# Expert blocks of a mixture-of-experts stage repacked by strips of 32 rows, with the next block's transposes moved to the middle of a block

## The chip, the cores and the metric

The kernel runs on one core of a Trainium2 chip. The metric is the device time of one execution in microseconds (us). Matmuls and transposes run on TensorE (PE in the profile), elementwise work on VectorE (DVE) and ScalarE (ACT), gathers and scatters of rows are issued by GpSimd (POOL), and SyncE (SP) issues the plain DMAs, the weight tiles among them, in the order of its program.

## The reference

Two transformer blocks in float32, one after the other, on 512 tokens of width 1024. The first ends in a mixture of experts, which is the stage that the change touches:

```
scores = sigmoid(h @ router_w)                        # 512 x 64
top_idx = top 6 of 64 experts, groups limited         # 3072 places
top_w = scores[top_idx] / sum * ROUTED_SCALE
for each expert e, over the tokens that chose it:
    y[tok] += top_w * ((silu(h @ w_gate[e]) * (h @ w_up[e])) @ w_down[e])
out = x + gt2 * (routed + swiglu(h, s_gate, s_up, s_down))   # the shared expert
```

The second block (state-space mixer, then a squared-relu MLP) follows and is not touched.

## The kernel before

**Places and blocks.** The 512 x 6 choices are sorted by expert into blocks of 128 row places. Four experts (60 to 63) have a fixed block each, blocks n = 0 to 3. The other 60 are ranked by load on the chip; a table `CAPS` says at compile time how many rows rank r may have. Ranks 0 to 17 stand alone (ranks 0, 1 and 2 over two blocks each), ranks 18 to 43 share a block in pairs (strips of 64 rows), ranks 44 to 59 in fours (strips of 32). That makes 42 blocks, whose order is that of `BLOCKS`, made by `plan()`: singles and shared blocks are interleaved. Rows beyond an expert's cap go to overflow blocks (`beyond`), of which there are none with these inputs.

**One block** (`ffn`): the block's 128 rows are gathered from DRAM into one of three buffers X; eight transposes (`pt_x` q = 0 and 1, four each) turn them, and `modulate` writes them as xT; 8 steps of matmuls make `gu` (512 columns) from weight tiles 0 and 1 of each expert, one matmul per strip and step; ACT and DVE make h; two transposes `pt_h`, and ACT copies them to hT; the matmuls `py` (two halves, two steps each) use weight tile 2; DVE multiplies into y, and POOL scatters y's rows, adding to `yacc` in DRAM. In the trace a block's tiles carry a b: gub, hb, pt_hb, pyb. Each float32 matmul is two records there, so a block with one expert has 16 gub and 8 pyb records, a pair 32 and 16, a four 64 and 32.

**Strips.** Where experts share a block, each has its own columns of the array by `tile_position=(0, a)`, a being the strip's first row.

**Weights.** Each expert is three tiles of 1024 KB (`ewrank` 0, 1, 2 and, by slot, `ewx`; the first four experts `ewfix`), which SP loads in block order into a ring of 10 to 13 slots, not before the slot's last reader is done, and with at most eight in flight (`load`). For the last `LEAVE` = 6 blocks three slots leave the ring.

**Hooks.** The shared expert's matmuls stand after the pyb of fixed block numbers: su, sg, su after n = 10, 11, 12, and `spy` after n = 13 to 16. After n = 17 the constants of the next stage are loaded (`row_g_final`, `sbc`, `ssd`) into space that slots of the ring held, and DVE computes with them.

**Order.** The order of instructions on an engine is decided by a scheduler unless the PE queue is pinned; SP runs its DMAs in program order.

Of the kernel before, what the change touches and what calls it, by code (L numbers as in the profile page):

```python
# [7 lines left out]
F32 = mybir.dt.float32  # L8
# [8 lines left out]
P = 128  # L17
# [809 lines left out]
def block_one(k, pool, early, two, route):  # L827
# [7 lines left out]
    with ExitStack() as es:  # L835
# [217 lines left out]
NE = 64  # L1053
NFIX = 4
NRK = NE - NFIX
NPAIR, NQUAD = 18, 44
CAPS = [256, 192, 152, 128, 124, 118, 108, 100, 92, 88, 86, 82, 79, 76, 75, 72, 70, 68, 64, 64, 62, 62, 59, 57, 56, 54, 54, 52, 51,
        50, 49, 46, 45, 44, 44, 43, 42, 41, 41, 40, 39, 38, 37, 37, 32, 32, 32, 31, 30, 30, 28, 26, 25, 23, 22, 20, 20, 18, 17, 16]
CAPS = [-(-c // 16) * 16 for c in CAPS]
NOV = 72  # L1060
LEAVE = 6
LAST = 0
AHEAD = 2
RING = 10
RINGX = 3

# [3 lines left out]

def plan():

    fixed = [(e, P, [("fix", NRK + e)]) for e in range(NFIX)]
    one, more, b, r = [], [], NFIX, 0
    while r < NRK:
        n = 1 if r < NPAIR else 2 if r < NQUAD else 4
        c = CAPS[r]
        if n == 1:
            g = []
            while c > 0:  # L1080
                g.append((b, min(c, P), [("rank", r)]))
                c -= P
                b += 1
            one.append(g)
        else:
            more.append([(b, P, [("rank", r + i) for i in range(n)])])
            assert max(CAPS[r:r + n]) <= P // n
            b += 1
        r += n

    more = more[::-1]
    m = len(one) - LAST
    order, i, j = [], 0, 0
    while i < m or j < len(more):
        if i >= m or j < len(more) and j * m <= i * len(more):
            order.append(more[j])
            j += 1
        else:
            order.append(one[i])
            i += 1  # L1100
    order += one[m:]
    return fixed + [x for g in order for x in g], b


BLOCKS, NB = plan()
NBT = NB + NOV
NSLOT = NB * P
STEP = [-(-c // P) * P if r < NPAIR else 64 if r < NQUAD else 32 for r, c in enumerate(CAPS)] + [P] * NFIX
CST2 = ["iota", "low", "col", "base", "cap"]


def const2():
    j = np.arange(P)[:, None]
    i = np.arange(P)[None, :]
    t = {
        "iota": np.broadcast_to(i, (P, P)),
        "low": (j < i),
        "col": np.broadcast_to(j, (P, P)),

        "base": np.broadcast_to(np.resize(np.concatenate([NFIX * P + np.cumsum([0] + STEP[:NRK - 1]), np.arange(NFIX) * P]), P)[:, None], (P, P)),  # L1120
        "cap": np.broadcast_to(np.resize(np.array(CAPS + [P] * NFIX), P)[:, None], (P, P)),
    }
    return np.concatenate([np.asarray(t[n], np.float32) for n in CST2], 1)
# [22 lines left out]
class Moe:  # L1146
# [332 lines left out]
    def fixed(self, ps, pp):  # L1479

        k, nc, rp = self.k, self.k.nc, self.rp
        V = nc.vector
        pl = rp.tile([P, 4, NFIX], F32, name="fx_pl")
        V.tensor_tensor(pl, pp[:, 0:4, NRK:NE], self.M[:, :, NRK:NE], ALU.mult)
        pt = ps.tile([P, NFIX, 4], F32, tag="tp", name="fx_tab")
        for e in range(NFIX):
            oh = self.part_of(512 * e, 4, P)
            V.tensor_tensor(oh, self.iota1.unsqueeze(1).to_broadcast([P, 4, P]), pl[:, :, e:e + 1].to_broadcast([P, 4, P]), ALU.is_equal)
            for t in range(4):
                nc.tensor.matmul(pt[:, e, :], oh[:, t, :], self.tv[:, t, e, :], start=(t == 0), stop=(t == 3))  # L1490
# [91 lines left out]
    def gather(self, idx):

# [5 lines left out]
                                            bounds_check=511, oob_is_err=False)  # L1589
        return X  # L1590

    def ffn(self, pool, ps, ws, X, wslot, n, nm):

        k, nc = self.k, self.k.nc
        xT = pool.tile([P, 8, P], F32, tag="xT", name="xT" + nm)
        for q in range(2):
            pt = ps.tile([P, 4, P], F32, tag="tp", name=f"pt_x{nm}{q}")
            for i in range(4):
                nc.tensor.transpose(pt[:, i, 0:n], X[0:n, (4 * q + i) * P:(4 * q + i + 1) * P], k.ident[0:n, 0:n])
            self.modulate(pt[:, :, 0:n], q, lambda c: xT[:, c, 0:n])  # L1600
        m = n // len(ws)
        parts = [(i * m, (i + 1) * m) for i in range(len(ws))]
        gu = ps.tile([P, 512], F32, tag="gu", name="gu" + nm)
        for i in range(8):
            for (a, b), w in zip(parts, ws):
                nc.tensor.matmul(gu[a:b, :], xT[:, i, a:b], w[i // 4][:, (i % 4) * 512:(i % 4) * 512 + 512],
                                 start=(i == 0), stop=(i == 7), **({"tile_position": (0, a)} if len(ws) > 1 else {}))
        sg = pool.tile([P, 256], F32, tag="sg", name="sg" + nm)
        nc.scalar.activation(sg[0:n], gu[0:n, 0:256], AF.Silu)  # L1609
        h = pool.tile([P, 256], F32, tag="h", name="h" + nm)  # L1610
        nc.vector.scalar_tensor_tensor(h[0:n], gu[0:n, 256:512], wslot[0:n], sg[0:n], ALU.mult, ALU.mult)  # L1611
        pt = ps.tile([P, 2, P], F32, tag="tp", name="pt_h" + nm)
        for c in range(2):
            nc.tensor.transpose(pt[:, c, 0:n], h[0:n, c * P:(c + 1) * P], k.ident[0:n, 0:n])
        hT = pool.tile([P, 2, P], F32, tag="hT", name="hT" + nm)
        nc.scalar.copy(hT[:, :, 0:n], pt[:, :, 0:n])
        y = pool.tile([P, 1024], F32, tag="y", name="y" + nm, bufs=3)
        for half in range(2):
            cs = slice(512 * half, 512 * half + 512)
            py = ps.tile([P, 512], F32, tag="py", name=f"py{nm}{half}")  # L1620
            for c in range(2):
                for (a, b), w in zip(parts, ws):
                    nc.tensor.matmul(py[a:b, :], hT[:, c, a:b], w[2][:, c * 1024 + half * 512:c * 1024 + half * 512 + 512],
                                     start=(c == 0), stop=(c == 1), **({"tile_position": (0, a)} if len(ws) > 1 else {}))
            nc.vector.tensor_tensor(y[0:n, cs], py[0:n], self.gt2[0:n, cs], ALU.mult)  # L1625
        return y

    def scatter(self, y, parts):

        for a, idx in parts:  # L1630
# [3 lines left out]
                                                in_=y[a:a + n], in_offset=None, bounds_check=511, oob_is_err=False,  # L1634
                                                compute_op=ALU.add)

    def blocks(self, bp, ps, hooks, span):

        pend, Xs = self.pend, self.Xs
        for n in range(*span):  # L1640
            b, rows, whos = BLOCKS[n]
            if n == len(BLOCKS) - LEAVE:
                for f in self.first:
                    self.slots.remove(f)
            if n == len(BLOCKS) - LAST:

                last = [self.load(w[0]) for _, _, w in BLOCKS[n:]]
                for i in ((0, 1), (2,)):
                    for w in last:
                        for j in i:  # L1650
                            w[1](j)
            ws = self.load_block(whos)
# [8 lines left out]
        if span[1] == len(BLOCKS):  # L1661
            for q in pend:
                self.scatter(*q)
            self.beyond(bp, ps)

    def beyond(self, bp, ps):
        k, nc, tc = self.k, self.k.nc, self.k.tc
        V = nc.vector
        n = nc.values_load(self.nov, min_val=0, max_val=NOV)
        with tc.For_i(0, n, 1) as i:  # L1670
# [747 lines left out]
def body(nc, tc, I, out, dbg=None):  # L2418
# [3 lines left out]
    with ExitStack() as es:  # L2422
# [11 lines left out]
        with ExitStack() as e1:  # L2434
            moe.es.close()
            moe.more_ring(e1, pool)
            bp = pool(e1, "moeb", 2)
            moe.Xt = [bp.tile([P, 1024], F32, name=f"X{i}", bufs=1) for i in range(AHEAD + 1)]
# [3 lines left out]
            for _, _, whos in BLOCKS[:3]:  # L2442
                moe.load_block(whos)
# [32 lines left out]
```

## Time and profile before

| | |
|---|---|
| three runs | 2032.37, 2032.55 and 2033.91 us |
| median | 2032.55 us |
| profiled execution | 2032.14 us |
| its span | 2030.3 us |
| mean granted clock of TensorE | 0.958 |
| PE busy | 1827.9 us (90%) |
| expert blocks, n = 4 to 41, on PE | 648.02 to 1215.35 us |
| bytes moved | 394.01 MB |

The span begins with the first instruction of the profiled execution and ends with the last; the profiled execution's own time is 1.84 us longer than its span. Times of the trace are counted from the span's start. The expert stage is some 30% of the span.

### The profile page before, as it was taken

How to read it: one execution, taken by the hardware profiler on the slowest of the kernel's cores; microseconds unless marked ns; L12 is line 12 of the kernel's file. 1: busy time of each engine (PE TensorE's matmuls, PEld its weight loads, DVE VectorE, ACT ScalarE, POOL GpSimd, SP SyncE). 2: the span in 40 equal slices, each digit the busy share in tenths (PEclk: the TensorE clock that was granted, in tenths of full speed). 3: DMA queues.
4: the chain of work that ended last, by engine and by line, in shares of the span. 5: the costliest groups of instructions: out<-in, count | busy, mean ns of one | idle time of the engine just before them, and what ended most of it. 6: DMA issues, size and time to landing. Idle time of an engine off the chain costs nothing. (4 is left out here: it accounts for less than half of the span.)

```text
span 2030.3 us, 24186 instructions
## 1 busy us (share of the span) xinstructions
PE 1827.9 (90%) x8465; PEld 1235.3 (61%) x8465; DVE 995.1 (49%) x2205; ACT 596.5 (29%) x1124; POOL 503.4 (25%) x408
## 2 busy tenths in 40 slices
PE   5997778987889999989999984999999999999998
PEld 3785556876644333333333333888888788888886
DVE  4789955667866222352222226667433453323352
ACT  5443311213323111111111114343323334323441
POOL 1314343542322221212121215333100113101300
PEclk9998888997979999999999996999999999999999
DMA  8354353226478999999999973333332432333241
GB/s 309 122 184 148 89 161 97 81 71 215 157 295 297 354 370 351 346 392 389 365 369 370 374 267 114 122 94 92 108 99 84 134 100 94 93 94 104 78 140 42
DMA packets 135569, 394.01 MB, mean 194 GB/s; under 512 B 46932, under 2 KB 59348, under 8 KB 109080
## 3 DMA queue, kind: packets, MB, share of 16 engines
q1 hardware_dynamic: 109608, 363.60, 50.6%
q0 software_dynamic: 12016, 27.29, 5.5%
q10 hardware_dynamic: 13824, 1.58, 0.5%
q8 instruction: 67, 1.10, 0.2%
q14 instruction: 54, 0.44, 0.1%
HBM read 365.13 MB, written 39.06 MB: 199 GB/s over the span
## 5 line engine op out<-in xcount | busy, mean ns | idle before, releaser
L139 PE MATMUL gub<-ewrank,xTb 128*64 128x512 f32 (+5 forms) x960 | 266.4, 595 | 0.8 <-DMA ewrank<-ew 0.2
L274 DVE TENSOR_TENSOR wlo<-wraw,whi 128x1024 fp32r<-128x1024 f32 (+1 forms) x103 | 120.9, 1174 | 138.4 <-ACT whi L273 137.5
L139 PEld LDWEIGHTS gub<-ewrank,xTb 128*64 128x64 f32 (+5 forms) x960 | 89.0, 140 | 159.5 <-issue 146.7
L273 ACT CAST whi<-wraw 128x1024 fp32r<-128x1024 f32 (+1 forms) x115 | 113.9, 991 | 211.9 <-PE psi L139 50.6
L139 PE MATMUL pyb<-ewrank,hTb 128*64 128x512 f32 (+5 forms) x440 | 154.6, 609 | 3.3 <-DMA ewrank<-ew 1.3
L139 PE MATMUL psi<-xnh,whi 128*128 128x512 f32 (+1 forms) x368 | 142.6, 388 | 0.0
L139 PE MATMUL psi<-xnl,whi 128*128 128x512 f32 (+1 forms) x368 | 141.1, 384 | 0.0
L1633 POOL DMA_INDIRECT yacc<-yb,tok x63 | 89.0, 1412 | 171.3 <-DVE yb L1625 121.5
L1611 DVE SCALAR_TENSOR_TENSOR hb<-gub,tw,sgb 128x256 f32<-128x256 f32 (+5 forms) x38 | 18.3, 482 | 230.8 <-ACT sgb L1609 230.8
L1335 ACT ACTIVATE xTb<-pt_xb,B,A 128x128 f32<-128x128 f32 (+5 forms) x168 | 74.1, 445 | 170.3 <-DVE xTb L1337 169.0
L139 PE MATMUL psi<-xnh,wlo 128*128 128x512 f32 (+1 forms) x296 | 113.2, 383 | 0.0
L1587 POOL DMA_INDIRECT X<-hrow,tok x38 | 39.5, 1041 | 292.0 <-PE pt_xb L142 286.4
L1337 DVE TENSOR_SCALAR xTb<-pt_xb,A,B 128x128 f32<-128x128 f32 (+5 forms) x168 | 65.6, 393 | 89.3 <-PE pt_xb L142 52.9
L2399 POOL TENSOR_TENSOR fr<-fr 128x512 f32<-128x512 f32 x32 | 48.6, 1519 | 238.2 <-ACT fr L2398 238.2
L139 PE MATMUL psf<-xml,whi 128*128 128x512 f32 (+1 forms) x272 | 102.5, 377 | 0.2 <-DVE xml L274 0.2
L139 PE MATMUL psf<-xmh,whi 128*128 128x512 f32 (+1 forms) x272 | 102.4, 377 | 0.2 <-ACT xmh L273 0.2
L139 PE MATMUL psf<-xmh,wlo 128*128 128x512 f32 (+1 forms) x272 | 102.4, 377 | 0.0
L1609 ACT ACTIVATE sgb<-gub 128x256 f32<-128x256 f32 (+5 forms) x42 | 16.0, 382 | 262.4 <-PE gub L139 262.4
L139 PEld LDWEIGHTS pyb<-ewrank,hTb 128*64 128x64 f32 (+5 forms) x440 | 46.7, 143 | 76.0 <-issue 64.7
L1625 DVE TENSOR_TENSOR yb<-pyb,gt 128x512 f32<-128x512 f32 (+5 forms) x84 | 58.0, 690 | 70.2 <-PE pyb L139 70.0
L139 PEld LDWEIGHTS psi<-xnh,whi 128*128 128x128 f32 x368 | 69.9, 191 | 13.8 <-ACT xnh L2264 0.4
L139 PEld LDWEIGHTS psi<-xnl,whi 128*128 128x128 f32 x368 | 70.0, 190 | 13.2
(752 smaller groups left out, 4026.0 us busy)
## 6 DMA issues: line engine op xcount, KB each, us to landing
ewrank<-ew SPq DMA_DIRECT2D x168, 1024.0 KB, 25.1
wraw<-w_in SPq DMA_DIRECT2D x59, 512.0 KB, 3.6
wraw<-ff SPq DMA_DIRECT2D x32, 512.0 KB, 3.5
wf<-ff SPq DMA_DIRECT2D x64, 256.0 KB, 2.7
wm<-w_mod SPq DMA_DIRECT2D x28, 512.0 KB, 7.8
ewfix<-ew SPq DMA_DIRECT2D x12, 1024.0 KB, 15.4
ewx<-ew SPq DMA_DIRECT2D x12, 1024.0 KB, 20.2
wm<-w_mod SPq DMA_DIRECT2D x10, 1024.0 KB, 6.2
```

Of the source, the lines that this page charges most:

```text
L139: return self._done(self.eng.matmul(out, lhsT, rhs, **kw), rate, rhs)
L273: nc.scalar.copy(hi, raw)
L274: (eng or nc.vector).tensor_tensor(lo, raw, hi.bitcast(F32), ALU.subtract)
L1335: nc.scalar.activation(dst(c), pt[:, i, :], AF.Identity, scale=sa, bias=sb)
L1337: nc.vector.tensor_scalar(dst(c), pt[:, i, :], sa, sb, ALU.mult, ALU.add)
L1587: self.k.nc.gpsimd.indirect_dma_start(out=X[0:idx.shape[0]], out_offset=None, in_=self.hrow, in_offset=bass.IndirectOffsetOnAxis(ap=idx, a ...
L1609: nc.scalar.activation(sg[0:n], gu[0:n, 0:256], AF.Silu)
L1611: nc.vector.scalar_tensor_tensor(h[0:n], gu[0:n, 256:512], wslot[0:n], sg[0:n], ALU.mult, ALU.mult)
L1625: nc.vector.tensor_tensor(y[0:n, cs], py[0:n], self.gt2[0:n, cs], ALU.mult)
L1633: self.k.nc.gpsimd.indirect_dma_start(out=self.yacc[self.nsc % 2], out_offset=bass.IndirectOffsetOnAxis(ap=idx, axis=0), in_=y[a:a + n], i ...
L2399: nc.gpsimd.tensor_tensor(r, r, r, ALU.mult)
```

## The change

**Packing.** Caps are multiples of 32: ranks 0 to 2 have 256, 192 and 160 rows, ranks 3 to 7 128, ranks 8 to 17 96, ranks 18 to 43 64, ranks 44 to 59 32. A rank of 96 shares its block with one of 32; as strips these are 64, 32 and 32 rows, the first two of one expert (three-strip blocks). Rank 1's last 64 rows share a block with rank 2's first 64, and rank 2's last 96 with rank 44. That leaves 39 blocks. Experts, weight tiles (64 times three), and the 3072 places are the same; the number of gathers falls from 42 to 39, and the row scatters stay at 67.

**Order of blocks.** After the fixed four: n = 4 one expert of 32 rows; 5, 6 rank 0; 7 a four; 8, 9 pairs; 10 to 12 ranks 1 and 2; 13 to 16 pairs; 17 rank 3; 18 to 20 pairs; 21 rank 4; 22 to 25 pairs; 26 rank 5; 27 to 29 three-strip; 30 rank 6; 31 to 34 three-strip; 35 rank 7; 36 to 38 three-strip. The hooks keep their block numbers. Up to n = 17 there are now 78 tiles to load, not 84, and for n from 18 on 114, not 108.

**Transposes.** The first four `pt_x` of block n + 1 are issued ahead of block n's `pt_h`, the other four behind it. PE runs in program order for the blocks from n = 2 on. Rows are gathered one block further ahead, with the same three buffers.

```
-NPAIR, NQUAD = 18, 44
+STRIPS = [8, 6, 5] + [4] * 5 + [3] * 10 + [2] * 26 + [1] * 16
+CAPS = [32 * s for s in STRIPS]
-NOV = 72
+NOV = 73
-AHEAD = 2
+AHEAD = 3
...
+    few += [group([0]), group([1, 2] + ones(1))] + [group([r]) for r in range(3, n4)]
+    for n in (3, 2, 1):
+        while any(STRIPS[r] == n for r in todo):
+            g = [r for r in todo if STRIPS[r] == n][:{3: 1, 2: 2, 1: 4}[n]]
+            many.append(group(g + (ones(1) if n == 3 else [])))
...
+    def turn(self, ps, xT, X, n, nm, q):
+        pt = ps.tile([P, 4, P], F32, tag="tp", name=f"pt_x{nm}{q}")
+        for i in range(4):
+            self.k.nc.tensor.transpose(pt[:, i, 0:n], X[0:n, (4 * q + i) * P:(4 * q + i + 1) * P], self.k.ident[0:n, 0:n])
+        return lambda: self.modulate(pt[:, :, 0:n], q, lambda c: xT[:, c, 0:n])
...
+        strips = [(a + i, min(a + m, a + i + s), w) for (a, m, _), w in zip(parts, ws)
+                  for i, s in ([(0, 64), (64, 32)] if m == 96 else [(0, m)])]
...
+        put = then.pop(0)() if then else None
         pt = ps.tile([P, 2, P], F32, tag="tp", name="pt_h" + nm)
         for c in range(2):
             nc.tensor.transpose(pt[:, c, 0:n], h[0:n, c * P:(c + 1) * P], k.ident[0:n, 0:n])
         hT = pool.tile([P, 2, P], F32, tag="hT", name="hT" + nm)
         nc.scalar.copy(hT[:, :, 0:n], pt[:, :, 0:n])
+        if put:
+            put()
+            then.pop(0)()()
...
+        self.k.nc.tensor.pin = span[0] > 0
...
+            nxt, xT = self.block_turns(bp, ps, n + 1) if n + 1 < len(BLOCKS) else ((), None)
+            y = self.ffn(bp, ps, ws, self.xT, (self.twf if n < NFIX else self.tw)[:, b:b + 1], rows, parts, f"b{b}", nxt)
```

How it moves PE's rows, first in a pair. Before, PE, from the `pt_h` of one pair block to the gub of the block after it:

```order
L142 MATMUL pt_hb35_7084<-cst_60,hb35_7082 128x128 x2
L142 MATMUL pt_xb140_7125<-cst_60,X0_4565 128x112 x4
L142 MATMUL pt_xb141_7134<-cst_60,X0_4565 128x112
L139 MATMUL pyb350_7090<-ewrank38_2_7037,hTb35_7087 64x512
L139 MATMUL pyb351_7096<-ewrank38_2_7037,hTb35_7087 64x512
L142 MATMUL pt_xb141_7134<-cst_60,X0_4565 128x112 x2
L139 MATMUL pyb350_7090<-ewrank39_2_7039,hTb35_7087 64x512
L139 MATMUL pyb350_7090<-ewrank38_2_7037,hTb35_7087 64x512
```

With the change, the same place of a pair block (ranks 40 and 41):

```order
L142 MATMUL pt_xb60_5615<-cst_60,X1_4566 128x128 x4
L142 MATMUL pt_hb35_5620<-cst_60,hb35_5613 128x128 x2
L142 MATMUL pt_xb61_5629<-cst_60,X1_4566 128x128 x4
L139 MATMUL pyb350_5639<-ewrank40_2_5586,hTb35_5623 64x512
L139 MATMUL pyb350_5639<-ewrank41_2_5588,hTb35_5623 64x512
L139 MATMUL pyb350_5639<-ewrank40_2_5586,hTb35_5623 64x512
L139 MATMUL pyb350_5639<-ewrank41_2_5588,hTb35_5623 64x512
L139 MATMUL pyb351_5645<-ewrank40_2_5586,hTb35_5623 64x512
```

The transposes of the next block left the pyb matmuls and stand around `pt_h`, and the two experts' strips alternate throughout, where two matmuls of one strip had followed each other.

A three-strip block with the change, PE, the first steps of gub and its middle (rank 9 with 96 rows, rank 46 with 32):

```order
L139 MATMUL gub15_8699<-ewrank9_0_8683,xTb15_8590 64x512
L139 MATMUL gub15_8699<-ewrank9_0_8683,xTb15_8590 32x512
L139 MATMUL gub15_8699<-ewrank46_0_8685,xTb15_8590 32x512
L139 MATMUL gub15_8699<-ewrank9_0_8683,xTb15_8590 64x512
L139 MATMUL gub15_8699<-ewrank9_0_8683,xTb15_8590 32x512
```

Before, PE, in a block with one expert of that size class:

```order
L139 MATMUL gub14_7143<-ewrank7_0_7115,xTb14_7124 112x512 x4
L139 MATMUL gub14_7143<-ewrank7_1_7117,xTb14_7124 112x512 x4
L142 MATMUL pt_hb14_7156<-cst_60,hb14_7154 128x112 x2
L142 MATMUL pt_xb340_7212<-cst_60,X1_4566 128x128 x4
L139 MATMUL pyb140_7162<-ewrank7_2_7119,hTb14_7159 112x512 x2
```

Where one matmul per step used the columns of the whole block, three now use 64, 32 and 32 of them, and a block has 24 gub matmuls instead of 8.

On SP, before, around the loads for the next stage (`row_g_final` to `ssd`) behind the tiles of n = 17:

```order
L1519 DMA ewrank5_2_6401<-ew 128x2048
L1728 DMA row_g_final_6459<-g_final 128x1024
L1820 DMA sbc_6469<-sbc 128x1024
L1822 DMA ssd_6471<-ssd 128x32
...
L1519 DMA ewrank40_0_6862<-ew 128x2048
```

With the change, the same place:

```order
L1522 DMA ewrank3_2_6372<-ew 128x2048
L1754 DMA row_g_final_6430<-g_final 128x1024
...
L1522 DMA ewrank30_0_6833<-ew 128x2048
L1522 ISA
L1522 DMA ewrank31_0_6835<-ew 128x2048
L1846 DMA sbc_6440<-sbc 128x1024
L1848 DMA ssd_6442<-ssd 128x32
L1522 ISA
L1522 DMA ewrank30_1_6837<-ew 128x2048
```

Two tiles of n = 18 now stand between `row_g_final` and `sbc`; the slot that `row_g_final` takes is last read by n = 15's pyb there, by n = 16's before; the tile `ewrank30_1` takes one that the last `spy` reads, as `sbc` does.

## Rows read from the trace of the kernel before

**Rows 1.** Windows of 50 us: engines' busy time, PEclk, DMA share, GB/s.

```profile
750.00:800.00 50.00, 46.64 (x197) 18.30 (x196) 10.23 (x20) 7.11 (x17) 8.74 (x7) 1.00 0.89 340
...
900.00:950.00 50.00, 46.72 (x170) 17.54 (x169) 12.67 (x26) 9.14 (x22) 12.24 (x10) 1.00 1.02 383
...
1100.00:1150.00 50.00, 46.20 (x165) 15.97 (x164) 11.43 (x24) 8.28 (x20) 12.45 (x10) 1.00 1.02 377
```

**Rows 2.** Waits of PE (856 to 1217 us): total, times, longest.

```profile
PE pt_hb L142 <- DVE hb L1611: 31.1, 25, 6.5
PE pyb L139 <- DMA ewrank<-ew: 1.3, 3, 0.7
```

**Rows 3.** Waits of SP's queue, 650 to 1220 us.

```profile
SPq L1519 <- DMA ewrank<-ew: 275.4, 117, 4.4
```

**Rows 4.** DMA of 855.5 to 1205 us: bytes and issues (KB, us to landing).

```profile
DMA packets 21950, 129.12 MB, mean 369 GB/s; under 512 B 4296, under 2 KB 4296, under 8 KB 8107
...
ewrank<-ew SPq DMA_DIRECT2D x108, 1024.0 KB, 25.6
```

**Rows 5.** PE's timeline, a pair block and a single (start, length).

```profile
901.48 1.45 PE L139 MATMUL pyb<-ewrank,hTb 128*112 128x512 f32 x3
902.77 0.60 PE L142 MATMUL pt_xb<-cst,X 128*128 128x128 f32 x4
903.30 7.09 PE L139 MATMUL gub<-ewrank,xTb 128*64 128x512 f32 x32
...
918.36 7.03 PE L139 MATMUL gub<-ewrank,xTb 128*112 128x512 f32 x16
926.39 0.41 PE L142 MATMUL pt_hb<-cst,hb 112*128 112x112 f32 x2 [1.00 <-DVE hb L1611]
...
927.29 3.69 PE L139 MATMUL pyb<-ewrank,hTb 128*112 128x512 f32 x8
930.82 0.60 PE L142 MATMUL pt_xb<-cst,X 128*128 128x128 f32 x4
931.35 1.08 PE L139 MATMUL gub<-ewrank,xTb 128*64 128x512 f32 x4
```

**Rows 6.** PE's timeline: n = 4's first matmuls, then n = 16 to its `spy`.

```profile
648.02 4.06 PE L139 MATMUL gub<-ewrank,xTb 128*32 128x512 f32 x35
...
840.09 7.09 PE L139 MATMUL gub<-ewrank,xTb 128*64 128x512 f32 x32
848.24 0.44 PE L142 MATMUL pt_hb<-cst,hb 128*128 128x128 f32 x2 [1.06 <-DVE hb L1611]
...
849.20 3.70 PE L139 MATMUL pyb<-ewx,hTb 128*64 128x512 f32 x16
852.83 3.70 PE L139 MATMUL spy<-ewshared,shh 128*128 128x512 f32 x8
```

**Rows 7.** SP's timeline around the loads for the next stage (start, length).

```profile
825.83 2.81 SPq L1519 DMA_DIRECT2D ewrank<-ew  x2
852.93 0.34 SPq L1728 DMA_DIRECT2D row_g_final<-g_final  x1
...
855.57 15.83 SPq L1519 DMA_DIRECT2D ewrank<-ew  x12
```

**Rows 8.** PE's timeline, n = 18.

```profile
883.42 0.69 PE L142 MATMUL pt_hb<-cst,hb 128*128 128x128 f32 x2 [6.48 <-DVE hb L1611]
...
884.97 5.07 PE L139 MATMUL pyb<-ewrank,hTb 128*64 128x512 f32 x16
```

**Rows 9.** A window of 4 us in n = 18, columns as in rows 1.

```profile
884.00:888.00 4.00, 4.00 (x14) 1.79 (x14) 3.11 (x9) 1.26 (x3) 0.00 (x0) 0.52 1.02 428
```

**Rows 10.** The tail: SP's last tiles, then PE's last block.

```profile
1174.34 8.20 SPq L1519 DMA_DIRECT2D ewrank<-ew  x4
...
1202.81 7.09 PE L139 MATMUL gub<-ewrank,xTb 128*80 128x512 f32 x16
...
1211.68 3.66 PE L139 MATMUL pyb<-ewrank,hTb 128*80 128x512 f32 x8 [0.44 <-ACT hTb L1616]
```

More of the change, by code (lines that the diff above doesn't have):

```diff
@@ L1071, in plan @@
 def plan():
[L1073 to L1096, printed above, removed]
+    few, many, base, todo = [], [], {}, list(range(NRK))
+    b = [NFIX]
+    def group(ranks):
+        g, at = [], 0
+        for r in ranks:
+            base[r], n = P * b[0] + at, CAPS[r]
+            todo.remove(r)
+            while n > 0:
+                if at % P == 0:
+                    g.append((b[0] + at // P, []))
+                m = min(n, P - at % P)
+                g[-1][1].append((at % P, m, ("rank", r)))
+                at, n = at + m, n - m
+        b[0] += len(g)
+        return [(i, max(a + n for a, n, _ in ps), ps) for i, ps in g]
@@ new lines, in plan @@
+    n4 = sum(s > 3 for s in STRIPS)
+    ones = lambda n: [r for r in todo if STRIPS[r] == 1][:n]
+    few += [group([0]), group([1, 2] + ones(1))] + [group([r]) for r in range(3, n4)]
[3 more added lines that the diff above has]
+            many.append(group(g + (ones(1) if n == 3 else [])))
+    many = many[::-1]
+    order, i, j = [(e, P, [(0, P, ("fix", NRK + e))]) for e in range(NFIX)], 0, 0
@@ L1097, in plan @@
+    while i < len(few) or j < len(many):
+        if i >= len(few) or j < len(many) and j * len(few) <= i * len(many):
+            order += many[j]
             j += 1
         else:
-            order.append(one[i])
+            order += few[i]
             i += 1
-    order += one[m:]
-    return fixed + [x for g in order for x in g], b
-BLOCKS, NB = plan()
+    return order, b[0], [base[r] for r in range(NRK)]
+BLOCKS, NB, BASE = plan()
 NBT = NB + NOV
 NSLOT = NB * P
-STEP = [-(-c // P) * P if r < NPAIR else 64 if r < NQUAD else 32 for r, c in enumerate(CAPS)] + [P] * NFIX
@@ L1571, in parts @@
     def parts(self, n):
-        b, rows, whos = BLOCKS[n]
+        b, rows, ps = BLOCKS[n]
         if n < NFIX:
             return [(0, self.tokf[0:rows, b:b + 1])]
-        if len(whos) == 1:
-            return [(0, self.tok[0:rows, b:b + 1])]
-        m = P // len(whos)
         t = {0: self.tok, 32: self.tok2, 64: self.tok3, 96: self.tok4}
-        return [(a, t[a][0:CAPS[r], b:b + 1]) for a, (_, r) in zip(range(0, P, m), whos)]
+        return [(a, t[a][0:m, b:b + 1]) for a, m, _ in ps]
     def gather(self, idx):
@@ L1590, in gather, with turns, ffn @@
         return X
-    def ffn(self, pool, ps, ws, X, wslot, n, nm):
-        k, nc = self.k, self.k.nc
[L1595 to L1602, printed above, removed]
+    def turn(self, ps, xT, X, n, nm, q):
[3 more added lines that the diff above has]
+        return lambda: self.modulate(pt[:, :, 0:n], q, lambda c: xT[:, c, 0:n])
+    def turns(self, pool, ps, X, n, nm):
+        xT = pool.tile([P, 8, P], F32, tag="xT", name="xT" + nm)
+        return [lambda q=q: self.turn(ps, xT, X, n, nm, q) for q in range(2)], xT
+    def ffn(self, pool, ps, ws, xT, wslot, n, parts, nm, then=()):
+        k, nc = self.k, self.k.nc
+        then = list(then)
+        strips = [(a + i, min(a + m, a + i + s), w) for (a, m, _), w in zip(parts, ws)
+                  for i, s in ([(0, 64), (64, 32)] if m == 96 else [(0, m)])]
         gu = ps.tile([P, 512], F32, tag="gu", name="gu" + nm)
         for i in range(8):
-            for (a, b), w in zip(parts, ws):
+            for a, b, w in strips:
                 nc.tensor.matmul(gu[a:b, :], xT[:, i, a:b], w[i // 4][:, (i % 4) * 512:(i % 4) * 512 + 512],
-                                 start=(i == 0), stop=(i == 7), **({"tile_position": (0, a)} if len(ws) > 1 else {}))
+                                 start=(i == 0), stop=(i == 7), **({"tile_position": (0, a)} if len(strips) > 1 else {}))
         sg = pool.tile([P, 256], F32, tag="sg", name="sg" + nm)
@@ L1635, in scatter, with block_turns, whole @@
                                                 compute_op=ALU.add)
+    def block_turns(self, bp, ps, n):
+        b, rows, _ = BLOCKS[n]
+        return self.turns(bp, ps, self.Xs[n], rows, f"b{b}")
+    def whole(self, bp, ps, n):
+        fs, xT = self.block_turns(bp, ps, n)
+        for f in fs:
+            f()()
+        return xT
     def blocks(self, bp, ps, hooks, span):
         pend, Xs = self.pend, self.Xs
+        self.k.nc.tensor.pin = span[0] > 0
         for n in range(*span):
-            b, rows, whos = BLOCKS[n]
+            b, rows, parts = BLOCKS[n]
             if n == len(BLOCKS) - LEAVE:
@@ L1644, in blocks @@
                     self.slots.remove(f)
[L1645 to L1652, printed above, removed]
-            self.rows_ahead(min(n + AHEAD, NFIX if span[0] == 0 else len(BLOCKS)))
-            y = self.ffn(bp, ps, ws, Xs[n], (self.twf if n < NFIX else self.tw)[:, b:b + 1], rows, f"b{b}")
+            ws = self.load_block([w for _, _, w in parts])
+            self.rows_ahead(min(n + AHEAD, NFIX if span[0] == 0 else len(BLOCKS)))
+            if n == 0:
+                self.xT = self.whole(bp, ps, n)
+            nxt, xT = self.block_turns(bp, ps, n + 1) if n + 1 < len(BLOCKS) else ((), None)
+            y = self.ffn(bp, ps, ws, self.xT, (self.twf if n < NFIX else self.tw)[:, b:b + 1], rows, parts, f"b{b}", nxt)
+            self.xT = xT
             part = self.parts(n)
@@ L1682, in beyond @@
             X = self.gather(sl)
-            y = self.ffn(bp, ps, [ws], X, sw, P, "o")
+            nxt, xT = self.turns(bp, ps, X, P, "o")
+            for f in nxt:
+                f()()
+            y = self.ffn(bp, ps, [ws], xT, sw, P, [(0, P, None)], "o")
             self.scatter(y, [(0, sl)])
@@ L2437, in body @@
             bp = pool(e1, "moeb", 2)
-            moe.Xt = [bp.tile([P, 1024], F32, name=f"X{i}", bufs=1) for i in range(AHEAD + 1)]
+            moe.Xt = [bp.tile([P, 1024], F32, name=f"X{i}", bufs=1) for i in range(AHEAD)]
             for t in moe.Xt:
```

17 lines of the change are left out of this document (7 added, 10 removed).

## The prediction

> **What bounds the kernel now.** PE is busy for 90% of the span, which invites the reading that every block taken from it shortens the run. So I read by stage. In the expert stage the windows show PE at 46 to 47 of 50 us throughout, but the DMA column changes: 0.89 and 340 GB/s while n is small, 1.02 and 377 to 383 GB/s in the later windows [rows 1]. There two resources are full at once. Next, who waits. PE hardly ever waits for a weight tile: behind 856 us its waits are 31.1 us for h, 25 times, and 1.3 us for tiles [rows 2]. SP in turn waits 275.4 us, 117 times, for a tile that is still landing, since only eight may be in flight [rows 3]. From issue to landing a tile takes 25.6 us (median) [rows 4]: a full queue. So behind 856 us tiles come just in time, and neither side has slack. Work taken from PE alone there turns into waits for tiles.
>
> In front of that lies a gate. SP's queue is in order; at 828.6 us it reaches `row_g_final`, which must wait until n = 16's pyb has let go of a slot, and issues it only at 852.93; the next weight tile goes at 855.57 [rows 7]. The last `spy` ends at 852.83 + 3.70 = 856.5 [rows 6]. Thus everything from n = 18 on, 108 tiles, is loaded behind about 856, in one full stretch: the last four tiles are issued from 1174.34 on in 8.20 us, so the last at about 1182, and with 23 to 25 us of flight it lands at about 1205 (my estimate from the median of 25.6, the queue being a little shorter at the end). The stretch is 1205 − 855.5 = 349.5 us and moves 129.12 MB at 369 GB/s [rows 4], 3.24 us per tile with the rows gathered and scattered beside it. PE's last pyb ends at 1211.68 + 3.66 = 1215.3, 10 us behind the last landing [rows 10].
>
> So the end of the stage is: gate + loading of the rest + PE's tail. I forecast these three; all behind the stage keeps its length.
>
> **The gate.** *A block on PE.* In a pair, gub to the next gub was 918.36 − 903.30 = 15.06 us; in a single 931.35 − 918.36 = 12.99 [rows 5]. What must stay: from gub's start to `pt_h` 8.15 us (pair, 840.09 to 848.24) or 8.03 (single); from `pt_h` to pyb, while ACT copies hT, 0.96 or 0.90; pyb to its end 3.63 or 3.53 [rows 5, 6]. Sums: 12.74 and 12.46, I take 12.6. The transposes cost nothing: the first four (0.60 us) fit in the 1.00 to 1.09 us that PE waits for h, the others where it waits for hT, as before. Without that cover a block would cost 0.6 us more, 13 × 0.6 = 8 us up to the gate. The remaining gain of a pair is the strips that alternate in pyb.
>
> *The thirteen blocks n = 4 to 16* took 856.5 − 648.0 = 208.5 us [rows 6], hooks included: four `spy` of 3.6 and three su or sg of 7.1, 35.4 us. Now 13 × 12.6 + 35.4 = 199.2, so −9.3; blocks 2 and 3 save some 0.5 each, −1. Against that n = 7, 8 and 9 need 24 tiles and n = 13 to 16 another 24, more than before in that time; at 3.24 us a tile 24 take 78 us, where the blocks and hooks of n = 13 to 16 last 4 × 12.6 + 14.4 = 65 us, and some ten filled slots cover the 13 us between. I put 2 us of waiting there, between 0 and 10. The gate: −8.3 us, bounds −10.3 and 0.
>
> **The rest to load.** The moved block order leaves 78 tiles up to n = 17 where 84 were, so 114, not 108, lie behind. Two of them now stand in SP's queue between `row_g_final`, which waits for n = 15's pyb, and `sbc`; they go before the last `spy` is done. Four more tiles than before remain: at 3.24 us each, rows included, 13 us, or at the best rate of the windows, 4 × 1.05 MB at 383 GB/s [rows 1], 11. I take 12. The three blocks fewer take three gathers away, but the same 3072 places are gathered and added, so bytes don't change.
>
> **PE behind the gate.** 22 blocks (n = 17 to 38) × 12.6 = 277 us against 362 of loading: PE waits some 85 us for tiles, 3.9 per block on average and about 6 in a block of two experts (6 tiles × 3.24 = 19.4). PE's saving here, 3 blocks of about 14 us and 2.3 per pair, is worth nothing.
>
> **The tail.** Before, PE still had a whole block to do behind the last landing, 10 us. Now PE has waited, and the last tile is a tile 2, which only pyb reads: 3.66 + 0.4 us. −6; bounds −6.5 and −2 (below).
>
> **Sum:** −8.3 + 12 − 6 = −2.3 us on the profiled 2032.14 (2030.3 of span and 1.84 around it) = 2029.8. The median shown is 0.4 above the profiled execution, so I say 2030.
>
> **What idle PE does to the clock.** At n = 18 PE stood 6.48 us for h, and behind it a pair's 16 pyb records took 5.07 us where 3.70 is usual [rows 8, 6]; the granted clock there was 0.52, the lower of its two levels (1.2 of 2.4 GHz) [rows 9]. Waits of about 6 us per block may do that each time. A block is then some 2 to 4 us longer, which the waits themselves absorb (12.6 + 4 is still under 19.4); only the last pyb counts, up to +3.7 us. That is the tail's bound of −2. The Trainium skill ("TensorE: Matmul & The Clock Gate", "HAM oscillation — how this bites in real kernels") describes just this, matmuls in bursts between waits for DMA that each start at the lower clock; n = 18 agrees.
>
> **Three-strip blocks** are not in the trace: matmuls of 64 and of 32 columns beside each other. Strips of one width do run side by side: a pair's 32 gub records take 7.09 us, a single's 16 take 7.03 [rows 5]. If that holds for mixed widths, gub costs 7.1. If the 64 wide strip and the two of 32 take turns, gub costs 14.2 and pyb 7.4. What rows show of a change of width: 128 wide behind 128 wide starts 0.16 us before the modelled end of the one before (901.48 + 1.45 against 902.77), 64 behind 128 only 0.07 (902.77 + 0.60 against 903.30; 930.82 + 0.60 against 931.35) [rows 5]. So a change costs some 0.1 us, which says nothing on running side by side. I take side by side, since every strip record shown does so, and keep the other as a rival. The Trainium skill ("TensorEngine Tiling (Array Packing)", "Key Properties") says that to change the tiling mode, not just the tile, drains the engine. By it each step would pay two drains and the widths would never overlap; the 0.1 us agrees that a change costs something, and the sum would be the third rival's.
>
> **Rivals.**
>
> *PE is the bound.* For it: its 1.3 us of waiting for tiles [rows 2]. Then PE's 1215.3 − 856.5 = 359 us behind the gate would become 277, −82, and with the gate −90: 1942. Against it: DMA share 1.02 [rows 1]. What DMA could give is the stretch at 383 GB/s, the best of the windows of 50 us, instead of 369: 337 us, −12 more than my sum, 2018. At 428, as in 4 us of n = 18 [rows 9], it would be −48 more, 1982, if gathers and scatters cost nothing, and I see no reason that they should cost less.
>
> *The gate does not move.* The pairs and fours now stand early, and if PE waits more than 10 us for their tiles before n = 16, the gate stays at 856: 0 + 12 − 6 = +6, and with a slow last pyb +9.7: 2038 to 2042. For it: 0.89 of DMA share in 750 to 800 us [rows 1], with a lighter load. Against: some ten slots are full when n = 4 starts. It decides from some 8 us of waiting on.
>
> *Mixed strips take turns* (slower, one mechanism). A three-strip block then costs 12.6 + 7.1 + 3.7 = 23.4 us, and with up to 48 changes at 0.1 us 28.2; that is above 19.4, the loading of its six tiles, from where it decides. Behind the gate 10 such blocks and 12 others take 385 to 433 us instead of 362, and n = 12 delays the gate by 11 to 15: +34 to +86 us, some 2064 to 2116; 2045 if they overlap in part.
>
> **Chances.** DMA binds behind the gate and the three terms hold, 2022 to 2038: 0.57. PE bound or better filled queue, under 2022: 0.08. Gate not moved, 2036 to 2045: 0.18. Strips in turns, over 2045: 0.17. A measurement can tell about 0.2%, 4 us. Faster than that, under 2028.5: 0.30 of the first and 0.08; same: 0.24 and 0.06; slower: 0.03, 0.12 and 0.17. The range that leaves about 2 in 10 out, most of it the long end of the strips' case, is 2019 to 2058; that of the likeliest alone 2022 to 2038.
>
> **What the next profile should show.** A pair from gub to gub, where tiles are there, 12.7 us, and `pt_xb` rows of 0.6 us ahead of and behind `pt_hb`. A three-strip gub (48 records) of about 7.1 us where no tile is waited for; 14 would mean turns. The last `spy` ending near 848. Behind it PE waiting some 85 us for `ewrank`, with PE's share down to about 40 of 50 or less (more where the clock is low), and DMA share still 1.0 at 365 to 385 GB/s. The last pyb ending within 4 to 8 us of the last landing, at about 1213. I am wrong if DMA moves clearly more than 383 GB/s for long, if DMA share falls below 0.95 between 870 and 1190, or if the gate is not within 845 to 857.

## The result and the profile after

| | before | changed |
|---|---|---|
| median | 2032.46 us (4 runs) | 2140.28 us (2138.60 to 2142.60, 4 runs) |
| ratio | | 1.0539, 95% interval [1.0525, 1.0552] |
| span of the profiled execution | 2030.3 us | 2137.9 us |
| last `spy`, n = 16, ends | 856.5 us | 877.4 us |
| last pyb ends | 1215.3 us | 1321.1 us |

The change makes the kernel 5.4% slower, where I forecast 2030 us and a range up to 2058. The stage ends 105.8 us later, the span is 107.6 us longer: nearly everything lies in the expert stage. Windows of the changed kernel, columns as in rows 1:

```profile
650.00:700.00 50.00, 46.14 (x186) 18.33 (x188) 22.81 (x126) 9.12 (x25) 10.06 (x8) 0.97 0.72 229
...
877.00:1036.00 159.00, 133.68 (x509) 50.60 (x508) 56.01 (x188) 24.41 (x60) 34.60 (x27) 0.98 1.01 388
1036.00:1321.00 285.00, 276.90 (x881) 60.97 (x880) 40.29 (x81) 29.24 (x70) 38.07 (x29) 1.00 0.72 251
```

From the gate to 1036 us, where pairs and singles stand, the picture is the predicted one: DMA at 1.01, PE waiting (busy for 134 of 159 us). From 1036 us on, where the ten three-strip blocks and two singles stand, it is turned over: PE busy for 277 of 285 us and DMA at 0.72 and 251 GB/s, against 1.02 and 377 before [rows 1]. And at 650 to 700 us DMA runs at 0.72 too. PE's timeline of the changed kernel: the pair n = 16, then one three-strip block (rows left out are other blocks):

```profile
861.02 7.09 PE L139 MATMUL gub<-ewrank,xTb 128*64 128x512 f32 x32
868.04 0.65 PE L142 MATMUL pt_xb<-cst,X 128*128 128x128 f32 x4
869.17 0.44 PE L142 MATMUL pt_hb<-cst,hb 128*128 128x128 f32 x2 [0.48 <-DVE hb L1620]
869.45 0.60 PE L142 MATMUL pt_xb<-cst,X 128*128 128x128 f32 x4
870.13 3.65 PE L139 MATMUL pyb<-ewrank,hTb 128*64 128x512 f32 x16
873.71 3.70 PE L139 MATMUL spy<-ewshared,shh 128*128 128x512 f32 x8
...
1152.77 15.95 PE L139 MATMUL gub<-ewrank,xTb 128*64 128x512 f32 x48
...
1170.76 8.01 PE L139 MATMUL pyb<-ewrank,hTb 128*64 128x512 f32 x24
1178.70 15.95 PE L139 MATMUL gub<-ewrank,xTb 128*64 128x512 f32 x48
```

The pair is what I predicted: 873.71 − 861.02 = 12.69 us from gub to what follows pyb, with four `pt_xb` on each side of `pt_hb`. The three-strip block takes 1178.70 − 1152.77 = 25.93 us; its gub 15.95, not 7.1, its pyb 8.01, not 3.65. There is no idle between the records of one gub: this is the matmuls' own pace, 1.99 us for each of its 8 steps. The records of the gub at 1152.77, grouped by the width of their strip (count, busy us, mean ns of one):

```profile
L139 PE MATMUL gub<-ewrank,xTb 128*64 128x512 f32 x16 | 8.6, 618 | 0.0
L139 PE MATMUL gub<-ewrank,xTb 128*32 128x512 f32 x32 | 8.4, 605 | 0.0
```

The two strips of 32 run side by side, since their 32 records take no longer than the 16 of the wide strip. The strip of 64 runs beside neither: 8.6 + 8.4 = 17.0 us, against 15.95 for the whole, and the 15 changes of width, at each of which a modelled end overlaps the next start by some 0.07 us, as in [rows 5], make up the difference.

### The profile page after: what moved, and what is told of

It reads as the page before. It is cut to its first block, busy times and chain, and to the rows that moved or that the text cites. A ratio compares the mean times of both kernels' runs of the same rounds, so it can differ in the third digit from the quotient of the medians.

```text
span 2137.9 us, 24580 instructions
## 1 busy us (share of the span) xinstructions
PE 1934.4 (90%) x8699; PEld 1230.8 (58%) x8699; DVE 986.5 (46%) x2184; ACT 585.5 (27%) x1106; POOL 504.2 (24%) x405
## 4 chain that ended last, share of the span: by engine, by line
PE 44%; issue 28%; DVE 9%; POOL 5%; DMA 3%; ACT 1%; POOLq 0%; SPq 0%; another core or an unknown queue 0%; DVEq 0%; ACTq 0%
PE psi L139 11%; PE pof L139 8%; PE psf L139 8%; POOL yacc L1646 3%; PE psco L139 2%; DVE cfa L746 2%; PE poo L139 2%; POOL X L1587 2%; DMA yacc<-yb,tok 2%; PE psga L139 1%; PE psgb L139 1%; PE pxca L139 1%; PE psy L139 1%; PE psp L139 1%; PE po L139 1%
## 5 line engine op out<-in xcount | busy, mean ns | idle before, releaser
L139 PE MATMUL gub<-ewrank,xTb 128*64 128x512 f32 (+2 forms) x1136 | 356.5, 612 | 22.4 <-DMA ewrank<-ew 22.4
L139 PEld LDWEIGHTS gub<-ewrank,xTb 128*64 128x64 f32 (+2 forms) x1136 | 89.9, 133 | 280.2 <-issue 238.1
L1620 DVE SCALAR_TENSOR_TENSOR hb<-gub,tw,sgb 128x256 f32<-128x256 f32 (+1 forms) x35 | 16.9, 483 | 353.7 <-ACT sgb L1618 353.7
L139 PE MATMUL pyb<-ewrank,hTb 128*64 128x512 f32 (+2 forms) x544 | 171.2, 608 | 5.2 <-DMA ewrank<-ew 2.1
L1618 ACT ACTIVATE sgb<-gub 128x256 f32<-128x256 f32 (+1 forms) x39 | 15.0, 384 | 538.5 <-PE gub L139 538.5
L1638 DVE TENSOR_TENSOR yb<-pyb,gt 128x512 f32<-128x512 f32 (+1 forms) x78 | 53.9, 691 | 117.9 <-PE pyb L139 117.8
L139 PEld LDWEIGHTS pyb<-ewrank,hTb 128*64 128x64 f32 (+2 forms) x544 | 41.1, 131 | 112.4 <-issue 96.4
L1340 DVE TENSOR_SCALAR xTb<-pt_xb,A,B 128x128 f32<-128x128 f32 (+1 forms) x156 | 62.1, 405 | 38.7 <-PE pt_xb L142 32.3
L139 PE MATMUL pof<-whi,fh 128*128 128x512 f32 x192 | 75.9, 396 | 0.0
```

The lines of the kernel that those rows point to most:

```text
L139: return self._done(self.eng.matmul(out, lhsT, rhs, **kw), rate, rhs)
L1340: nc.vector.tensor_scalar(dst(c), pt[:, i, :], sa, sb, ALU.mult, ALU.add)
```

## The experiments

**e1, one width of strips.** The disputed cost by itself: 96 rows as three strips of 32.

```
-                  for i, s in ([(0, 64), (64, 32)] if m == 96 else [(0, m)])]
+                  for i, s in ([(0, 32), (32, 32), (64, 32)] if m == 96 else [(0, m)])]
```

> One edit to the changed kernel: a rank of 96 rows is three matmul strips of 32 rows instead of 64 + 32, so a block of 96 + 32 has four strips of one width. Theory: strips of different widths take turns on the array, strips of one width run side by side. Then gub of such a block takes 7.1 us (64 records) instead of 15.95, pyb 3.65 instead of 8.01, the block 12.6 instead of 25.9, and the stage is bound by DMA again. The time then shows how good the rest of the sum was: 2030 us if the gate moves as predicted, about 2045 if PE's waits for tiles at n = 8 to 10, which the changed kernel shows, stay (last spy near 864 us, 362 us of loading, 4 us of tail). Rival: every matmul of a strip costs 0.33 us of its own, whatever its width (15.95 / 48 records); then four strips take 21 us in gub and the run is slower than the changed kernel's, about 2200. Second rival: the moved transposes and the pinned queue cost the time; then it stays above 2100.

Measured: 2045.67 us, ratio to before 1.0070 [1.0051, 1.0090]. Its timeline, a block of ranks 2 and 44, the last `spy` and the last pyb:

```profile
780.12 7.07 PE L139 MATMUL gub<-ewrank,xTb 128*32 128x512 f32 x64
...
789.26 3.64 PE L139 MATMUL pyb<-ewrank,hTb 128*32 128x512 f32 x32
...
861.62 3.70 PE L139 MATMUL spy<-ewshared,shh 128*128 128x512 f32 x8
...
1223.53 5.06 PE L139 MATMUL pyb<-ewrank,hTb 128*32 128x512 f32 x26 [0.68 <-DMA ewrank<-ew]
```

More matmuls (64 records for 48), and gub falls from 15.95 to 7.07 us. So it is not the number of matmuls, nor the moved transposes, which e1 keeps: 95 of the 108 us are the mixed widths. The rest, some 15 us above my sum, stays; the last `spy` ends at 865.3, as expected for the case in which the gate stays late.

**e2, mixed widths grouped.** All 64 wide matmuls of a block's gub, then all 32 wide ones; likewise in each half of pyb.

```
-        for i in range(8):
-            for a, b, w in strips:
+        for i, (a, b, w) in [(i, q) for f in (64, 32) for i in range(8) for q in strips if q[1] - q[0] == f] if len(strips) == 3 else [(i, q) for i in range(8) for q in strips]:
...
```

> One edit to the changed kernel: in a three-strip block all matmuls of the 64 wide strip are issued first and those of the two 32 wide strips behind them (in pyb for each half), so the width changes once per accumulation instead of twice per step. Theory: widths take turns, and a change costs about 0.07 us by itself; gub 14.2 us instead of 15.95, pyb 7.4 instead of 8.01, 2.3 us less per block, 11 blocks: about 2115 us. Rival: it is the change of width that costs (0.5 us each, a drained array) and not the turns; with one change gub comes near 7.5 to 8 us and the time near 2040.

Measured, in one run and so without an interval: 2113.4 us (before 2029.8 on the same chip; the four runs of the changed kernel lie within 4 us). Its timeline, the end of one such block and the next:

```profile
1138.64 14.07 PE L139 MATMUL gub<-ewrank,xTb 128*64 128x512 f32 x48
...
1154.76 7.47 PE L139 MATMUL pyb<-ewrank,hTb 128*64 128x512 f32 x24
1162.16 14.07 PE L139 MATMUL gub<-ewrank,xTb 128*64 128x512 f32 x48
```

14.07 us is twice 7.03, the gub of a single [rows 5]: the widths take turns even with one change between them. The 8 steps of a gub in the changed kernel make 15 changes of width, where e2 makes one: the other 14 cost (15.95 − 14.07) / 14 = 0.134 us each. In pyb 7 changes became 3, and (8.01 − 7.47) / 4 = 0.135 us. The rival, in which only the change costs, falls. By itself e2 leaves a doubt, since it puts all matmuls of the wide strip ahead of the others; that the widths take turns also where they alternate is read from the records of the changed kernel above.

**e3, the old packing with the new order of transposes.** The plan of the kernel before, with its strips, in the changed kernel.

```
-STRIPS = [8, 6, 5] + [4] * 5 + [3] * 10 + [2] * 26 + [1] * 16
+NPAIR, NQUAD = 18, 44
...
```

> The packing of the kernel before (42 blocks, strips of one width in each, its order of blocks and tiles) with the change's transposes around the middle, pinned PE queue and rows gathered three ahead. Theory: the new order takes about 2.3 us from a pair on PE and 0.5 from a single; up to the gate (n = 4 to 16) that moves the gate by some 10 us, and the same 108 tiles follow, so the stage ends 10 to 15 us earlier: 2017 to 2023. Rival: the pinned order makes PE wait in line for tiles or rows that the scheduler had worked around; then 2033 or more.

Measured: 2032.09 us, 1.0016 [1.0007, 1.0026]. The forecast of 2017 to 2023 failed. PE's timeline in the four at n = 14, and the last `spy`:

```profile
813.40 1.05 PE L139 MATMUL pyb<-ewrank,hTb 128*32 128x512 f32 x2 [1.44 <-DMA ewrank<-ew]
816.55 1.06 PE L139 MATMUL pyb<-ewrank,hTb 128*32 128x512 f32 x1 [2.11 <-DMA ewrank<-ew]
...
854.89 3.70 PE L139 MATMUL spy<-ewshared,shh 128*128 128x512 f32 x8
```

What PE saved in front of the gate it spent at the fours' tiles, in waits (5.6 us up to the gate) and in slower matmuls behind them (granted clock 0.93 from 800 to 850 us, before 1.00); the last `spy` ended at 858.6, 2 us later than before, although n = 4 had begun at 643.7, 4.3 us earlier. In that order of blocks tiles are just in time before the gate as well.

**e4, strips of 32 with the old order of transposes** (at the head of their own block, PE not pinned, rows two ahead).

```
-AHEAD = 3
+AHEAD = 2
...
-        self.k.nc.tensor.pin = span[0] > 0
+        self.k.nc.tensor.pin = False
...
-            nxt, xT = self.block_turns(bp, ps, n + 1) if n + 1 < len(BLOCKS) else ((), None)
...
+            xT = self.whole(bp, ps, n)
...
```

> The new packing with strips of 32 (as in the first run), but the transposes at the head of their own block, an unpinned PE queue and rows gathered two ahead, as in the kernel before. Theory: behind the gate DMA is the bound, so the order costs only what it delays the gate, some 2.3 us for each of the 7 pairs and 0.5 for each of the others in front of it, and what is left of PE's tail: 10 to 25 us over the first run, 2040 to 2065. Rival: the new order is worth nothing where DMA binds; then it is equal to the first run within 4 us.

Measured: 2052.36 us, 1.0116 [1.0092, 1.0139], 6.7 us above e1: less than expected, but not nothing. Its last `spy` and its last pyb:

```profile
864.26 3.70 PE L139 MATMUL spy<-ewshared,shh 128*128 128x512 f32 x8
...
1226.12 5.09 PE L139 MATMUL pyb<-ewrank,hTb 128*32 128x512 f32 x32 [0.52 <-ACT hTb L1626]
```

The `spy` ends at 868.0, 2.6 us later than in e1; from there to the end of the last pyb both take 363.3 us.

**e5 and e6, the order of blocks.** What did e1 lose? From 650 to 700 us its DMA moved 227 GB/s, the changed kernel's 229. That window of the kernel before, which rows 1 leave out:

```profile
650.00:700.00 50.00, 45.40 (x192) 19.47 (x184) 13.33 (x33) 10.05 (x25) 13.89 (x11) 1.00 1.00 368
```

SP's timeline of the changed kernel there, and what SP waited for from 655 to 702 us:

```profile
655.99 5.75 SPq L1522 DMA_DIRECT2D ewrank<-ew  x2
662.95 0.34 SPq L1844 DMA_DIRECT2D lam<-lam  x1
677.83 15.93 SPq L1522 DMA_DIRECT2D ewrank<-ew  x4
694.00 2.03 SPq L1522 DMA_DIRECT2D ewx<-ew  x2
```

```profile
SPq L1522 <- PE gub L139: 24.7, 6, 13.7
SPq L1522 <- PE pyb L139: 11.7, 2, 6.9
```

SP stood for slots that PE had not read yet: n = 4 to 6 use six tiles in 41 us of PE (648.91 to 689.78 us; the expectations below miscount them as nine), so the ring is full and DMA idles; behind them come the four and two pairs with 24 tiles, and PE waits. Two other orders of the same blocks in e1. In e6 this line is the only edit to e1:

```
-    many = many[::-1]
+    many, few = many[::-1], few[::-1]
```

In e5 the light blocks come late and between heavy ones:

```
...
+    for g in (many[1:9] + many[:1] + many[9:12] + few[:1] + many[12:15] + few[1:2] + many[15:16] + few[2:3] + many[16:18]
+              + few[3:4] + many[18:20] + few[4:5] + many[20:22] + few[5:6] + many[22:24] + few[6:7] + many[24:]):
+        order += g
```

> The first run (strips of 32) with another order of blocks, nothing else: behind the fixed four come the four and seven pairs at once, and the light blocks (rank 59 alone, rank 0's two, ranks 1 and 2's three, ranks 3 to 7) stand later, each between heavy ones. Theory: what the first run lost against the sum (15 us) is DMA time before the gate: n = 4 to 6 need 9 tiles in 37 us of PE, the ring is full, SP waits for slots, and 650 to 700 us moved 227 GB/s where the kernel before moved 368, 7 MB or 19 us of loading. With heavy blocks first DMA stays full, the gate comes later (PE waits for tiles) but with fewer tiles behind it, and the stage ends some 18 us earlier: about 2027. Rival: the place of the gate decides (the last spy's end plus the tiles behind it); a later gate then makes it slower, 2055 or more. Second rival: the time is lost to TensorE's lower clock in the waits; PE waits no less here, so 2046 again.

> The first run with one edit: the list of light groups is taken from its other end, so n = 4 and 5 are light (ranks 59 and 7), n = 6 is the four, and ranks 0 to 2 with their five blocks come at n = 27 to 35. Theory: half of the idle DMA time of the first run is avoided (two light blocks first and not three, of six tiles and not nine in 37 us): about 8 us less than the first run, 2037. Rivals as in the run before: 2046 where the order of blocks doesn't matter.

Measured: e5 2033.29 us, 1.0009 [0.9998, 1.0020]; e6 2026.39 us, 0.9970 [0.9956, 0.9984]. Both are faster than e1 (12 and 19 us), so the order of blocks was what e1 lost; but which of the two is better I had the wrong way round. In e5 a new hole opened at the gate. Its window of 850 to 900 us and the wait behind it:

```profile
850.00:900.00 50.00, 46.62 (x154) 19.87 (x152) 32.69 (x189) 7.69 (x20) 9.15 (x7) 0.97 0.67 234
```

```profile
SPq L1518 <- PE spy L139: 29.4, 1, 29.4
```

PE had waited for the heavy blocks' tiles and came late to the hooks; SP stood at the gate for 29.4 us, until the last `spy` ended at 878.9. The rival of e5's expectation, that a later gate costs, held in part.

**e7, spread.** Blocks ordered from both findings: heavy ones where the ring would be full, light ones where PE would wait, a single one last.

```
...
+    seq = [many[1], few[6], many[2], many[0], many[3], few[5]] + many[4:8] + [few[4]] + many[8:12] + [few[0]] + many[12:14] + [few[3]]
+    seq += many[14:16] + [few[1]] + many[16:] + [few[2]]
+    for g in seq:
+        order += g
```

> Strips of 32 as in the first run, and an order of blocks that follows from the runs so far: the four at n = 4, then ranks 7, 42/43, 59, 40/41, 6, six pairs with rank 5 among them up to n = 16, rank 0's two light blocks at n = 19 and 20 where PE waits for tiles anyway, ranks 1 and 2 at n = 26 to 28, heavy blocks to the end, and the single rank 3 last. Theory: the run with the singles taken from the other end still left DMA at 0.93 in 650 to 700 us and 0.88 in 1150 to 1200, some 9 us, and its last block had two row scatters one behind the other; with both mended the time falls by 6 to 10 us more, to 2017 to 2021. Rival: DMA is already as full as it gets; then 2026 again.

Measured: 2018.51 us, 0.9940 [0.9924, 0.9955], the fastest of all. Windows of e7, its last `spy` and its last pyb:

```profile
650.00:700.00 50.00, 44.58 (x197) 15.92 (x186) 12.62 (x34) 9.19 (x24) 14.01 (x11) 1.00 1.02 394
750.00:800.00 50.00, 48.25 (x198) 18.26 (x196) 9.91 (x21) 7.70 (x19) 8.86 (x7) 1.00 1.01 399
850.00:900.00 50.00, 38.47 (x142) 13.98 (x139) 31.45 (x135) 4.90 (x12) 10.76 (x8) 0.93 1.01 403
```

```profile
850.56 3.70 PE L139 MATMUL spy<-ewshared,shh 128*128 128x512 f32 x8
...
1194.99 3.70 PE L139 MATMUL pyb<-ewrank,hTb 128*128 128x512 f32 x8 [0.52 <-ACT hTb L1623]
```

DMA is nearly full from 650 us on and through the gate (0.95 at the lowest, in the windows left out from 800 and from 900 us); the last `spy` ends at 854.3 and the last pyb at 1198.7, 16.6 us before that of the kernel before. In this order 90 tiles stand up to n = 17, where e1 has 78, so fewer are left to load behind the gate.

**e8, only a single last.** e6 with rank 3's block at the end.

> The run with the singles taken from the other end, with one edit: rank 3's block, one expert and one row scatter, is moved from n = 23 to the last place, n = 38. Theory: from y's end to the next stage's first load it took 10.3 us there and 5.7 us in the kernel before, since a block of two experts ends in two scatters one behind the other; a single at the end saves 4.5 us of that and costs about 2.5 us of PE behind the last landing, so 2024. Rival: the scatter is hidden behind other work of the next stage; then 2026 to 2029.

Measured: 2024.31 us, 0.9966 [0.9954, 0.9978]; the intervals of e6 and e8 overlap, so the two are not told apart. In the profiled executions the ends themselves can't be compared either: with the same code up to there, n = 4 begins at 649.2 us in e6 and at 643.9 in e8. What can be is the gap behind the last pyb. In e6 the last pyb ends at 1206.1 and the load of the sums starts at 1217.0, in e8 at 1201.0 and 1210.1, in the kernel before 1215.3 and 1221.8: the gap shrank by about 2 of the 4.5 us that it was longer than before. What the rest is stays open.

**e9, the old packing, light blocks spread.** e3 with the singles from the other end and ranks 2, 1, 0 in the middle.

```
-    more = more[::-1]
+    more, one = more[::-1], one[:10:-1] + one[2::-1] + one[10:2:-1]
```

> The packing of the kernel before (42 blocks, no new strips) with the change's order of transposes, and the light blocks spread as in the spread order: fours among the first, ranks 2, 1 and 0 with two blocks each at n = 22 to 29, rank 3 last. It asks what the new packing is worth beside the order. Theory: where DMA is the bound, three blocks fewer on PE are worth little; most of the gain of the spread order comes without them, 2019 to 2026. Rival: the 38 blocks of the old packing (479 us of PE and 35 of hooks) leave PE too little slack, and the time stays at that of the old packing in its old order, 2030 to 2034.

Measured: 2037.79 us, 1.0038 [1.0026, 1.0050]: the rival held, and more. Its window of 950 to 1000 us has DMA at 0.89 and PE at 47.5 of 50, as if PE, with three blocks more, were the bound there. But this order also has e5's hole at the gate, with the last `spy` ending at 894.0:

```profile
850.00:900.00 50.00, 48.09 (x171) 18.62 (x171) 19.09 (x58) 6.96 (x18) 8.68 (x7) 1.00 0.73 257
```

Which of the two costs how much is not shown. One order is not the best order, so it doesn't give the packing's worth by itself.

**e10, spread with the old order of transposes** (e4's edit in e7).

> The spread order with strips of 32, but transposes at the head of their own block, PE unpinned, rows two ahead. Theory: as between the first and the fourth run, the order of transposes is worth some 7 us where DMA binds, since it keeps the gate early: 2025. Rival: nothing, since PE waits for tiles almost everywhere with this order of blocks: 2018 to 2021.

Measured: 2029.59 us, 0.9998 [0.9987, 1.0009], 11 us above e7, more than the 7 expected. Waits of PE, 640 to 1230 us, e10 and below it e7:

```profile
PE pt_hb L142 <- DVE hb L1617: 52.4, 36, 13.7
PE gub L139 <- DMA ewrank<-ew: 12.2, 8, 2.1
```

```profile
PE gub L139 <- DMA ewrank<-ew: 31.7, 17, 2.9
PE pt_hb L142 <- DVE hb L1617: 26.8, 36, 7.5
```

With the new order PE is early enough to wait for tiles; with the old one it stands 26 us longer for h, and SP's queue waits 122.3 us for gub to free slots, in e7 55.3. The end of e10's last `spy` and its last pyb:

```profile
864.68 2.84 PE L139 MATMUL spy<-ewshared,shh 128*128 128x512 f32 x6
...
1209.90 3.70 PE L139 MATMUL pyb<-ewrank,hTb 128*128 128x512 f32 x8 [0.52 <-ACT hTb L1623]
```

The loss lies in front of the gate: the last `spy` ends at 867.5, 13 us later than in e7 (n = 4 began 3 us later), while from there to the end of the last pyb it is 346.1 us, in e7 344.4.

## Why the prediction was wrong, by its own steps

**Three-strip blocks: the step that failed.** "I take side by side, since every strip record shown does so" was a generalisation from strips of one width to strips of two: gub was priced at 7.1 us and took 15.95, the block 25.93 and not 12.6. The rows could not decide it, and I said so, but gave the other answer 0.17. That rival named the mechanism and nearly the size: 23.4 to 28.2 us a block by prediction, 25.93 measured. (Its 48 changes of width were too many: 8 steps of gub and 4 of pyb make 24 with the ends. The row that I read as 128 columns behind 128 has 112 in front, so it is a change of width too, and gave no price.) The rival put the time at 2064 to 2116, and 2140 came. One reason is that its sum set PE's 385 to 433 us, 410 with the 25.93 measured, against one stretch of DMA, where 1321.1 − 877.4 = 443.7 us came. In fact the stretch falls in two: from 877 to 1036 us pairs and singles, where DMA binds, and from 1036 us on the three-strip blocks, where PE binds; one part's slack cannot help the other. The other reason is the gate, 14 us or more later than the rival had it. The Trainium skill ("TensorEngine Tiling (Array Packing)", "Key Properties") says that a change of tiling mode drains the engine. The trace agrees that the two widths don't overlap, and e2 prices a change at 0.13 us; most of the cost is the lost overlap (14.07 against 7.07 us), not the changes.

**The gate: wrong sign.** I said −8.3 us within −10.3 and 0; without the mixed widths (e1) it came +8.8 late (865.3 against 856.5), in the changed kernel +20.9, of which 13.3 is the three-strip block at n = 12. Some 3 of e1's 8.8 us are the start: n = 4 begins at 648.0 us before and at 650.9 in e1, and e6 and e8, alike up to there, differ by 5 us. From n = 4's start to the last `spy` my sum had 201.2 us, with the 2 of waiting (its hooks add up to 35.7, not 35.4, which changes nothing); the kernel before took 208.5 and e1 214.4. In e1 the two pairs n = 8 and 9, behind the full ring, took 17.2 and 19.1 us instead of 12.7. I had set the tiles needed against the time in which they are needed, but not asked when DMA may load them: with light blocks first the ring is full and loading time is lost. e5 to e7 show that the order of blocks costs or gives that much; the changed order gave 78 tiles up to n = 17 and idle DMA, the worst of those tried with the new packing.

**The rest to load: right, once the widths are one.** From e1's last `spy` at 865.3 to its last pyb's end at 1228.6 are 363 us, where loading and tail had 362 + 4.

**PE's saving behind the gate is worth nothing: right.** The order of transposes is worth 6.7 us in e4 against e1 and 11 us in e10 against e7, but not behind the gate: from there to the end of the last pyb both of the first pair take 363.3 us, and the other two 346.1 and 344.4. It is the gate that moves, as the sum had it, by 2.6 and by 13 us in the profiled executions. In e3 it didn't move: there tiles were late in front of the gate, and the saving went into waits. That a gain on PE shows only where the order of blocks has brought the tiles in time is my reading of these pairs; it is argued, not shown. The transposes hidden for nothing, and a pair of 12.7 us, were right too.

**DMA's best rate.** I took 383 GB/s as the best of windows of 50 us; e7 reaches 394 to 403 in the windows shown, and e1 400 and 398 from 900 to 1000 us; the later windows of both, from 1000 to 1150 us, have 363 to 382. Why the rates differ is not shown. So 2018, which I had priced as the end of the rival in which PE is the bound, is reached by e7 and need not be the floor.

**The clock.** PE did fall to the lower level behind waits for tiles and for h: in e1's last pyb the mean granted clock was 0.76 from 1225 to 1228 us, and its last 26 records took 5.06 us, where all 32 took 3.64 at n = 12. That is within the bound on the tail; that the clock didn't decide elsewhere fits the 363 us, but no run varied it.

## What to carry to other kernels

Strips of 64 and of 32 columns did not run side by side here, strips of one width did: cut all of a packed matmul's strips to the narrowest, even if one operand is then used by several strips. Where two resources are both full, ask for each stretch when the prefetcher may load, not only how much: a run of light blocks fills the ring and idles DMA, a run of heavy ones starves PE, and the same blocks in another order were worth 27 us here (e7 against e1). A trace that lacks an operation does not speak for the cheap answer; price the dear one by its own rows and weigh it by what it would do.

## What the runs showed of the hardware that was not expected

Two strips of 32 columns and one of 64 took 14.07 us grouped (e2) and 15.95 alternating, where four strips of 32 took 7.07 (e1): the array shared by these two widths worked on one of them at a time. A change between them costs 0.13 us, in gub and in pyb alike; at the ends of blocks the rows of before had suggested 0.1.
